# Opening loads in the order in which they land, and the last shift group formed by VectorE from transposed weights

## The chip, the cores and the metric

The kernel runs on one core of a Trainium2 chip. A core has engines that run side by side, each through its own list of instructions in order: TensorE (PE in the profile; PEld is its weight load), VectorE (DVE), ScalarE (ACT), GpSimd (POOL) and SyncE (SP), which here only issues transfers. Transfers run on 16 DMA engines. The metric is the time of the device for one execution, in microseconds (us), as the median of several.

## The reference

One layer of a diffusion backbone for 256 latent tokens `x` with 256 context tokens `ctx`, width 2048. What matters here is its head: each stream is normalised, scaled and shifted by columns that come from a conditioning vector, and then projected.

```python
def modulate(x, g, shift, scale):
    return rms_norm(x, g) * (1 + scale) + shift
...
mod_x = jnp.split((jax.nn.silu(c) @ w_mod[l] + b_mod[l])[:, None, :], 6, axis=-1)
mod_c = jnp.split((jax.nn.silu(c_ctx) @ w_mod[l] + b_mod[l])[None, None, :], 6, axis=-1)
...
qa, ka, va, qb, kb, vb, rb, gf, gb, gate_a, gate_b = proj(modulate(x, g_mix[l], mod_x[0], mod_x[1]))
... = proj(modulate(ctx, g_mix[l], mod_c[0], mod_c[1]))
```

Part 0 of `mod` is the shift, part 1 the scale, each of 2048 channels and for two vectors (`c` for the latent stream, `c_ctx` for the context). `proj(h)` is `h @ w_in`, 2048 by 13344. After it follow windowed attention, gated linear attention, the merge, and a ConvFFN, none of which the change touches.

## The kernel before

Channels lie on partitions: 2048 channels are 16 tiles of 128 (`KT = 16`), and a tile of the normalised input is 128 channels by 256 tokens. Every product is made of three: weights and inputs are split into a high part (`whi`, written by ScalarE, L211) and a remainder (`wlo`, formed by VectorE from the weights and `whi`, L212); high times high, high times low and low times high are summed.

The head of the kernel goes through the 16 channel tiles in five groups: `GROUPS = [(0, 2), (2, 2), (4, 4), (8, 4), (12, 4)]`. For a group, the shift and scale columns of its channels must be there (`mods`), then the input is scaled (`affine_scale`, VectorE) and shifted and split (`affine_shift`: ScalarE writes `h..hi` at L511, VectorE writes `h..lo` at L512), and then TensorE multiplies the group's rows of `w_in` for the q block of the linear attention (`QB`, two projections of 512 columns, latent tokens only), the k block (`KB`, both streams) and the v block (`VB`, both streams). Sums go on over the groups: what a projection leaves in its bank is added by VectorE to `qb`, `kb` or `vb` (L521), and a bank can be used again when that is done. Weights come in chunks of 256 rows by 512 columns (512 KB, a buffer `raw` of a pool of seven). A group of four tiles has eight chunks: QB 1 to 4, KB 5 and 6, VB 7 and 8. For a chunk TensorE first does the products with `whi`, then those with `wlo`.

Shift and scale of a group are computed while the products of the group before run (for the first group, in the opening). One part of one group is `mod_both`: TensorE multiplies the vectors `cS` (32 columns, of which two are used) with `w_mod`, in steps of one 1 MB buffer `mraw` each, four steps for a group of four tiles, into a bank `pm`; VectorE transposes it (`mtr`, L335), TensorE gathers it into columns (`pcol`), VectorE copies those (L345) and adds the bias (L348). Such steps stand in a list, `bg_steps`, and are taken up at the start of chunks at a given rate. While the second group's products run, the places are written out instead (`steps`, `also`, `mid`). `mraw` and the arrays of the head share a pool of 16 buffers (`M`), of which six are left for `mraw` up to the fourth group and two in it.

All these loads are issued by SP in one chain (`load`), in the order in which the program asks for them, and each waits until its buffer is free. In the opening, `pack` (constants, biases and the two vectors in one array) and `crow` (the vector as rows) are issued from ScalarE's queue. Everything that starts needs `pack`: the identity for TensorE's warming transposes (`idle`), and the vectors for `cS`.

For other parts of `mod` (2 to 5) the kernel already has a second way, `mod_latent`: VectorE multiplies a tile of transposed weights (128 channels by 1024) with the vector as a row on all partitions (`csrow`, read back from `csd`) and sums along the row (L376).

A scheduler of the recording layer sets the order on each engine from dependencies and its own estimates. `in_order` and `pin` add orders without a wait.

Of the kernel before, what the change touches and what calls it, by code (L numbers as in the profile page):

```python
# [16 lines left out]
P = 128  # L17
D = 2048
# [13 lines left out]
def layer_kernel(ctx, tc, A, out):  # L32
# [17 lines left out]
    def M(name, shape, dt=F32):  # L50
        return big.tile(shape, dt, name=name, tag="M")
# [62 lines left out]

    pack = cst.tile([P, 322], F32, name="pack")
    nc.scalar.dma_start(pack, A["k_pack"])
    crow = sm.tile([KT, P], F32, name="crow", tag="t128", bufs=2)
    nc.scalar.dma_start(crow, A["k_crow"])
    ident, c1, sel = pack[:, 0:128], pack[:, 128:256], pack[:, 256:290]
# [17 lines left out]
    csd = dram.tile([KT, P], F32, name="csd")  # L137
    G.dma_start(csd, crow)
# [174 lines left out]
    def mod_both(part, t0, n, dst, put=None):  # L313
# [5 lines left out]
        def step(k0):  # L319
            if k0 == 0:  # L320
                a.append(bank(f"pm{part}_{t0}", (P, w), side=True))
            raw = M("mraw", [P, nk, w])
            src = A["w_mod01"][part, t0 + k0 // nk].rearrange("p (c d) -> p c d", c=nk)
            if t0 < 4 and part == 0 and k0:
                load(raw[:, 0:nk // 2, :], src[:, 0:nk // 2, :])
                load(raw[:, nk // 2:nk, :], src[:, nk // 2:nk, :])
            else:
                load(raw, src)
            for k in range(nk):
                kt = k0 + k  # L330
                q = 32 * (kt % 4)
                mm_b(a[0][q:q + 32, :], cS[:, kt, :], raw[:, k, :], start=(kt < 4), stop=(kt >= 12))
            if k0 == KT - nk:
                tr = W2("fb", "mtr", [P, n, 4, 32])
                folded[:] = [V.transpose(tr.rearrange("p a b c -> p (a b c)"), a[0]).ins]  # L335
                a.append(tr)
                if put is not None:
                    put(end)
# [14 lines left out]
    def mod_latent(parts, begin=None):  # L353
# [16 lines left out]
        def step(i):  # L370
# [8 lines left out]
            if begin is not None and i == 0:  # L379
# [27 lines left out]
    def rms_scale(ss, n, shape):  # L407
# [16 lines left out]
            for (t0, n), put in zip(groups, [None, None] + [lambda fn: pend.append(fn)] + 2 * [lambda fn: defer(0, fn)])]  # L424
    pend = []

    rrow1 = []
    kbt = M("kb0", [P, 4, 512])
    vb0 = M("vb0", [P, 4, 512])

    def square_sums(s):
# [3 lines left out]
        for i in range(4):  # L435
# [6 lines left out]
            else:  # L442
                V.tensor_tensor(q, x_, x_, op=ALU.mult)
                parts.extend(q[:, k, :] for k in range(4))
# [97 lines left out]
    V.tensor_scalar(gm1, gmix, -0.5, None, op0=ALU.mult)  # L542
# [73 lines left out]
    for gi, (t0, n) in enumerate(groups):  # L616
# [8 lines left out]
        if gi + 1 < len(groups):  # L625
            bg_steps.extend(mods[gi + 1][0] + mods[gi + 1][1])
            ticks = 4 * ((n + 1) // 2)
            bg_rate[:] = [1.4 * len(bg_steps) / ticks + 0.01, 0.0]
            if gi == 1:
                bg_rate[:] = [0.0, 0.0]  # L630
                steps = iter([1, 2, 1, 4, 0, 0])

# [8 lines left out]

                also = iter([next_columns] * 3 + [scale_2, next_columns, lambda: affine_shift(0, *groups[2])])

# [722 lines left out]
```

## Time and profile before

| | us |
|---|---|
| median of 3 runs | 1973.95 (1973.88 to 1974.18) |
| the profiled execution | 1973.72 |
| its span, first to last instruction | 1972.0 |
| TensorE busy in the span | 1952.8 |
| TensorE busy from 0 to 24 us | 16.21 |

In the profile a row of the timeline or of the chain starts with its time from the start of the span. `xN` is the number of instructions in it; one matrix product in 32-bit floats shows as two of them, so a step of four products of `mod_both` is a row of `pm` x8. What stands behind `<-` in square brackets ended the idle time of the engine just before. TensorE's busy time includes ends that are modelled, so a busy TensorE is not one at its peak.

### The profile page before, as it was taken

The numbers are of one execution on the slowest core, as the hardware profiler recorded it, in microseconds if no ns is written. First come the engines' busy times: TensorE is split into PE (matmuls) and PEld (weight loads), VectorE is DVE, ScalarE is ACT, GpSimd is POOL, SyncE is SP. The second block draws the span as 40 slices with busy tenths as digits, with TensorE's granted clock in tenths as the row PEclk, the third lists the DMA queues.
The fourth block names the chain that finished last, engine by engine and source line by source line (L and its number), as shares of the span: only waits on it lengthen the run. The fifth ranks groups of instructions, "written<-read, shape, count | busy, mean of one in ns | idle before, by whom it ended". The sixth has DMA issues, their size and how long they took to land.

```text
span 1972.0 us, 27091 instructions
## 1 busy us (share of the span) xinstructions
PE 1952.8 (99%) x10304; PEld 1635.6 (83%) x10304; DVE 1396.9 (71%) x2150; ACT 971.6 (49%) x1415; POOL 39.9 (2%) x60
## 2 busy tenths in 40 slices
PE   8999999999999999999999999999999999999999
PEld 6679988888887777888888888888888888888887
DVE  5756855785768998777776467989886545677754
ACT  5223655462346565444444445755555334555533
POOL 0010000020000000000000000000000000000000
PEclk9999999999999999999999999999999999999999
DMA  9975222226654466899997677688786556666563
GB/s 392 412 255 176 69 66 71 79 84 210 212 162 126 129 208 220 297 299 307 312 310 237 238 246 252 193 276 284 263 275 224 192 193 191 186 188 191 188 212 114
DMA packets 182867, 420.90 MB, mean 213 GB/s; under 512 B 12512, under 2 KB 12736, under 8 KB 177744
## 3 DMA queue, kind: packets, MB, share of 16 engines
q1 hardware_dynamic: 181200, 413.45, 63.7%
q0 software_dynamic: 1360, 5.54, 1.0%
q8 instruction: 81, 1.33, 0.3%
q14 instruction: 50, 0.41, 0.1%
q10 hardware_dynamic: 176, 0.17, 0.0%
HBM read 416.98 MB, written 2.13 MB: 213 GB/s over the span
## 4 chain that ended last, share of the span: by engine, by line
PE 94%; DVE 3%; ACT 1%; DMA 1%; issue 1%; ACTq 0%; DVEq 0%
PE acc L83 72%; PE accs L83 12%; PE pa L95 2%; PE poa L95 1%; PE pS L95 1%; PE po L95 1%; PE pm L95 1%; DVE wlo L212 1%; PE ptp L98 1%; DMA mraw<-in_w_mod 1%; ACT whi L211 0%; DVE q L831 0%; PE pto L98 0%; DMA pack<-in_k_pack 0%; DVE k L838 0%
## 5 line engine op out<-in xcount | busy, mean ns | idle before, releaser
L212 DVE TENSOR_TENSOR wlo<-raw,whi 128x1024 fp32r<-128x1024 f32 x568 | 694.0, 1223 | 426.5 <-ACT whi L211 387.8
L211 ACT ACTIVATE whi<-raw 128x1024 fp32r<-128x1024 f32 x568 | 601.1, 1059 | 785.1 <-PE acc L83 605.0
L83 PE MATMUL accs<-h,whi 128*128 128x512 f32 x704 | 176.3, 392 | 0.0
L83 PE MATMUL acc<-h,whi 128*128 128x512 f32 x640 | 160.4, 392 | 0.0
L83 PEld LDWEIGHTS accs<-h,whi 128*128 128x128 f32 x704 | 126.6, 189 | 22.6
L83 PE MATMUL acc<-whi,h01hi 128*128 128x512 f32 x352 | 139.7, 397 | 0.0
L83 PE MATMUL acc<-whi,h00hi 128*128 128x512 f32 x352 | 139.2, 395 | 0.0
L83 PE MATMUL acc<-whi,h01lo 128*128 128x512 f32 x352 | 138.4, 393 | 0.0
L83 PE MATMUL acc<-whi,h00lo 128*128 128x512 f32 x352 | 137.6, 391 | 0.0
L83 PE MATMUL acc<-whi,al 128*128 128x512 f32 x352 | 137.0, 389 | 0.0
L83 PE MATMUL acc<-whi,ah 128*128 128x512 f32 x352 | 137.0, 389 | 0.0
L83 PEld LDWEIGHTS acc<-h,whi 128*128 128x128 f32 x640 | 115.1, 189 | 20.6
L83 PEld LDWEIGHTS accs<-h,wlo 128*128 128x128 f32 x704 | 96.0, 190 | 6.9
L83 PE MATMUL acc<-wlo,h01hi 128*128 128x512 f32 x352 | 99.0, 396 | 0.0
L83 PE MATMUL accs<-h,wlo 128*128 128x256 f32 x704 | 98.2, 282 | 0.0
L83 PE MATMUL acc<-wlo,h00hi 128*128 128x512 f32 x352 | 98.1, 394 | 0.0
L83 PE MATMUL acc<-wlo,ah 128*128 128x512 f32 x352 | 94.3, 389 | 0.0
L83 PEld LDWEIGHTS acc<-h,wlo 128*128 128x128 f32 x640 | 87.4, 190 | 6.3
L83 PE MATMUL acc<-h,wlo 128*128 128x256 f32 x640 | 89.4, 282 | 0.0
L376 DVE CUSTOM_DVE_ANT_0 raw<-raw,csrow,pack 128x1024 f32<-128x1024 f32 x64 | 81.2, 1278 | 0.0
L83 PEld LDWEIGHTS acc<-whi,al 128*128 128x128 f32 x352 | 66.1, 188 | 13.7
L83 PEld LDWEIGHTS acc<-whi,ah 128*128 128x128 f32 x352 | 66.1, 188 | 13.7
(376 smaller groups left out, 3553.0 us busy)
## 6 DMA issues: line engine op xcount, KB each, us to landing
raw<-in_w_in SPq DMA_DIRECT2D x204, 512.0 KB, 4.5
raw<-in_w_up SPq DMA_DIRECT2D x176, 512.0 KB, 4.2
raw<-in_w_modT SPq DMA_DIRECT2D x128, 512.0 KB, 4.6
raw<-in_w_down SPq DMA_DIRECT2D x88, 512.0 KB, 3.6
mraw<-in_w_mod SPq DMA_DIRECT2D x30, 1024.0 KB, 12.5
raw<-in_w_attn_o SPq DMA_DIRECT2D x32, 512.0 KB, 5.3
raw<-in_w_gla_o SPq DMA_DIRECT2D x32, 512.0 KB, 5.4
raw<-in_w_out SPq DMA_DIRECT2D x32, 512.0 KB, 4.4
```

The source lines that it names most:

```text
L83: r = pe_seq(PE.matmul(*a, **k))
L95: return pe_seq(after(PE.matmul(*a, **k)))
L98: return pe_seq(after(PE.transpose(*a)))
L211: j = S.activation(hi[:, 0:n, :], raw[:, 0:n, :], AF.Copy).ins
L212: i = V.tensor_tensor(lo[:, 0:n, :], raw[:, 0:n, :], hi[:, 0:n, :].bitcast(F32), op=ALU.subtract).ins
L376: i0 = V.tensor_tensor_reduce(out=raws[i], in0=raws[i], in1=row[0], scale=1.0, scalar=d if h else bmod[:, b0:b0 + 1], op0=ALU.mult, op1=AL ...
```

## The change

Opening. The vectors get a small array of their own, `ccol`, which is issued first, then `crow` (now with both vectors, 32 rows), then `pack` without the vectors. The 1 MB loads of the first two groups' shift are no longer cut in halves. The first half of the first scale (`a0`) stands ahead of the last three sums of squares instead of behind `factor_row`. 14 of the 32 warming transposes are left out (`idle`).

Second group. Of the four `mod_both` steps of the third group's shift that stood in one place, the last stands one place later, and so does its gathering.

Third and fourth group. The fifth group's shift (channel tiles 12 to 15) is not formed by `mod_both` any more, but by `shift_rows`: for each half of the 2048 input rows, both vectors are read as rows onto all partitions (`c2row`, two transfers of 512 KB into an `M` buffer), and for each of the four tiles a 512 KB tile of transposed weights is loaded into a `raw` buffer and multiplied and summed by VectorE twice, once per vector. The first half stands among the third group's products, the second among the fourth's.

```diff
-    pack = cst.tile([P, 322], F32, name="pack")
+    ccol = cst.tile([P, KT, 2], F32, name="ccol")
+    nc.scalar.dma_start(ccol.rearrange("p k s -> p (k s)"), A["k_ccol"])
+    crow = sm.tile([2 * KT, P], F32, name="crow", tag="t128", bufs=2)
+    nc.scalar.dma_start(crow, A["k_crow"])
+    pack = cst.tile([P, 290], F32, name="pack")
     nc.scalar.dma_start(pack, A["k_pack"])
-    crow = sm.tile([KT, P], F32, name="crow", tag="t128", bufs=2)
-    nc.scalar.dma_start(crow, A["k_crow"])
...
-    S.activation(cS[:, :, 0:2], pack[:, 290:322].rearrange("p (k s) -> p k s", s=2), AF.Silu)
+    S.activation(cS[:, :, 0:2], ccol, AF.Silu)
...
             raw = M("mraw", [P, nk, w])
-            src = A["w_mod01"][part, t0 + k0 // nk].rearrange("p (c d) -> p c d", c=nk)
-            if t0 < 4 and part == 0 and k0:
-                load(raw[:, 0:nk // 2, :], src[:, 0:nk // 2, :])
-                load(raw[:, nk // 2:nk, :], src[:, nk // 2:nk, :])
-            else:
-                load(raw, src)
+            load(raw, A["w_mod01"][part, t0 + k0 // nk].rearrange("p (c d) -> p c d", c=nk))
...
+    def shift_rows():
+        rows = []
+        def half(h):
+            rows[:] = [M("c2row", [P, 2, 1024])]
+            for s in range(2):
+                k = s * KT + 8 * h
+                load(rows[0][:, s, :], csd[k:k + 8, :].rearrange("k p -> (k p)").partition_broadcast(P))
+        def step(h, j):
+            raw = wr.tile([P, 2, 512], F32, name="raw", tag="raw").rearrange("p a b -> p (a b)")
+            prod = f2.tile([P, 1024], F32, name="prod", tag="mod", bufs=1)
+            load(raw, A["w_modT0"][h, j - 12])
+            for s in range(2):
+                d = shift1[:, s, j:j + 1]
+                i = V.tensor_tensor_reduce(out=raw if s else prod, in0=raw, in1=rows[0][:, s, :], scale=1.0,
+                                           scalar=d if h else bmod[:, j:j + 1],
+                                           op0=ALU.mult, op1=ALU.add, accum_out=d).ins
+                in_order(last_lo[0], i)
+        return [[lambda h=h: half(h)] + [lambda h=h, j=j: step(h, j) for j in range(12, 16)] for h in range(2)]
...
-    idle(10)
+    idle(8)
     pr, add_up = square_sums(0)
     add_up(0, 6)
...
+    a0()
     add_up(6, 9)
     factor_row(pr)
-    a0()
-    idle(6)
     a1()
-    idle(4)
+    idle(2)
     ea()
     b0()
     affine_scale(0, *groups[0])
-    idle(6)
+    idle(4)
     b1()
...
-            bg_steps.extend(mods[gi + 1][0] + mods[gi + 1][1])
+            if gi < 2:
+                bg_steps.extend(mods[gi + 1][0] + mods[gi + 1][1])
+            elif gi == 2:
+                first, both = by_rows.pop(0), mods[3][0] + mods[3][1]
+                bg_steps.extend(first[0:1] + both[0:4])
+                for pair in zip(first[1:], both[4:]):
+                    bg_steps.extend(pair)
+            else:
+                first, both = by_rows.pop(0), mods[4][0]
+                bg_steps.extend(first[0:1])
+                for pair in zip(both, first[1:]):
+                    bg_steps.extend(pair)
...
-                steps = iter([1, 2, 1, 4, 0, 0])
+                steps = iter([1, 2, 1, 3, 1, 0])
```

What this moves shows in the order of the built programs. First place: TensorE at the end of the second group, from the last `whi` products of its KB chunk to the start of the third group (`pm_4` is the third group's shift, `pm_8` the fourth's scale). Before:

```order
L95 MATMUL pm_4_693<-mraw,cS 32x512 x16
L83 MATMUL acc<-h00hi,wlo 128x256
...
L83 MATMUL acc<-h10hi,wlo 128x256
L95 MATMUL pcol_4_740<-mtr,pack 32x32
L83 MATMUL acc<-whi,h00hi 128x512
...
L83 MATMUL acc<-wlo,h00hi 128x512 x4
L83 MATMUL acc<-wlo,h10hi 128x512 x4
L95 MATMUL pm_8_793<-mraw,cS 32x512 x4
```

and of the change:

```order
L95 MATMUL pm_4_681<-mraw,cS 32x512 x12
L83 MATMUL acc<-h00hi,wlo 128x256
...
L83 MATMUL acc<-h10hi,wlo 128x256
L95 MATMUL pm_4_681<-mraw,cS 32x512 x4
L83 MATMUL acc<-whi,h00hi 128x512
...
L95 MATMUL pcol_4_752<-mtr,pack 32x32
L83 MATMUL acc<-wlo,h00hi 128x512 x4
L83 MATMUL acc<-wlo,h10hi 128x512 x4
L95 MATMUL pm_8_784<-mraw,cS 32x512 x4
```

The fourth step of `pm_4` now stands behind the KB chunk's `wlo` products, and the gathering behind the VB chunk's `whi` products. At the same place, ScalarE; the last of the `whi` ahead of the `h00hi` is, before, that of the third group's first chunk. Before:

```order
L511 ACTIVATE h10hi<-xr_87,shift_101 128x256 x2
L211 ACTIVATE whi<-raw 128x1024 x3
L511 ACTIVATE h00hi<-xr_85,shift_101 128x256 x4
L511 ACTIVATE h10hi<-xr_87,shift_101 128x256 x4
L211 ACTIVATE whi<-raw 128x1024 x7
```

and of the change:

```order
L534 ACTIVATE h10hi<-xr_89,shift_103 128x256 x2
L213 ACTIVATE whi<-raw 128x1024 x2
L534 ACTIVATE h00hi<-xr_87,shift_103 128x256 x4
L534 ACTIVATE h10hi<-xr_89,shift_103 128x256
L213 ACTIVATE whi<-raw 128x1024
L534 ACTIVATE h10hi<-xr_89,shift_103 128x256 x3
```

The first chunk's `whi` now stands behind five writes of `h..hi`, which wait for the gathered shift.

Second place: VectorE in the third group, from the sums of its first QB block into `qb` to the `wlo` of the fourth chunk. Before:

```order
L521 TENSOR_TENSOR qb_252<-qb_252,acc 128x512
L521 TENSOR_TENSOR qb_253<-qb_253,acc 128x512
L335 STREAM_TRANSPOSE mtr<-pm_8_793 128x512
L212 TENSOR_TENSOR wlo<-raw,whi 128x1024
L345 COPY scale_102<-pcol_8_914 32x2x4 x4
L348 TENSOR_TENSOR scale_102<-scale_102,pack 128x2x4
L499 SCALAR_TENSOR_TENSOR scale_102<-scale_102,gm_100 128x4 x2
L502 SCALAR_TENSOR_TENSOR xr_86<-xr_86,scale_102,rrow 128x256 x2
L212 TENSOR_TENSOR wlo<-raw,whi 128x1024
```

and of the change (the ISA rows of `prod` and `raw` are the new multiply-and-sums, the ISA rows with `shift_103` alone the reading of the sum), up to the third chunk's `wlo`:

```order
L544 TENSOR_TENSOR qb_241<-qb_241,acc 128x512
L544 TENSOR_TENSOR qb_242<-qb_242,acc 128x512
L401 ISA prod,shift_103<-raw,c2row,pack 128x1024
L401 ISA shift_103 128x1
L332 STREAM_TRANSPOSE mtr<-pm_8_784 128x512
L401 ISA raw,shift_103<-raw,c2row,pack 128x1024
L401 ISA shift_103 128x1
L214 TENSOR_TENSOR wlo<-raw,whi 128x1024
```

and from there to the fourth chunk's:

```order
L342 COPY scale_104<-pcol_8_910 32x2x4 x4
L345 TENSOR_TENSOR scale_104<-scale_104,pack 128x2x4
L401 ISA prod,shift_103<-raw,c2row,pack 128x1024
L401 ISA shift_103 128x1
L522 SCALAR_TENSOR_TENSOR scale_104<-scale_104,gm_102 128x4 x2
L401 ISA raw,shift_103<-raw,c2row,pack 128x1024
L401 ISA shift_103 128x1
L525 SCALAR_TENSOR_TENSOR xr_88<-xr_88,scale_104,rrow 128x256 x4
L525 SCALAR_TENSOR_TENSOR xr_90<-xr_90,scale_104,rrow 128x256 x4
L214 TENSOR_TENSOR wlo<-raw,whi 128x1024
```

Two multiply-and-sums stand ahead of each of these two `wlo`, and all eight scalings of `xr` (before: two) ahead of the second.

Third place: VectorE in the fourth group, of the change, from the `wlo` of its fourth chunk to the sums of the second QB block:

```order
L214 TENSOR_TENSOR wlo<-raw,whi 128x1024
L401 ISA prod,shift_103<-raw,c2row,shift_103 128x1024
L401 ISA shift_103 128x1
L401 ISA raw,shift_103<-raw,c2row,shift_103 128x1024
L401 ISA shift_103 128x1
L214 TENSOR_TENSOR wlo<-raw,whi 128x1024
L544 TENSOR_TENSOR qb_243<-qb_243,acc 128x512
L544 TENSOR_TENSOR qb_244<-qb_244,acc 128x512
```

and before:

```order
L212 TENSOR_TENSOR wlo<-raw,whi 128x1024
L502 SCALAR_TENSOR_TENSOR xr_86<-xr_86,scale_102,rrow 128x256 x2
L502 SCALAR_TENSOR_TENSOR xr_88<-xr_88,scale_102,rrow 128x256 x2
L521 TENSOR_TENSOR qb_254<-qb_254,acc 128x512
L521 TENSOR_TENSOR qb_255<-qb_255,acc 128x512
```

The sums of the second QB block, which free the banks of the KB chunks, stood right behind four scalings; now two multiply-and-sums and a `wlo` stand ahead of them.

More of the change, by code (lines that the diff above doesn't have):

```diff
@@ L136, in layer_kernel @@
         S.preload_act_table_set("natural_log_exp_and_others")
-    csd = dram.tile([KT, P], F32, name="csd")
+    csd = dram.tile([2 * KT, P], F32, name="csd")
     G.dma_start(csd, crow)
@@ L425, in layer_kernel @@
     pend = []
+    by_rows = shift_rows()
     rrow1 = []
@@ L429, in layer_kernel @@
     vb0 = M("vb0", [P, 4, 512])
+    squared = []
     def square_sums(s):
@@ L442, in square_sums @@
             else:
-                V.tensor_tensor(q, x_, x_, op=ALU.mult)
+                squared.append(V.tensor_tensor(q, x_, x_, op=ALU.mult).ins)
                 parts.extend(q[:, k, :] for k in range(4))
@@ L640, in scale_2, with shift_2 @@
                         affine_scale(s, *groups[2])
-                also = iter([next_columns] * 3 + [scale_2, next_columns, lambda: affine_shift(0, *groups[2])])
+                def shift_2():
+                    next_columns()
+                    affine_shift(0, *groups[2])
+                also = iter([next_columns] * 3 + [scale_2, next_columns, shift_2])
                 def mid():
@@ L1345 @@
     c, c_ctx = data.pop("c")[0], data.pop("c_ctx")
-    data["k_crow"] = c.reshape(KT, P)
+    data["k_crow"] = np.concatenate([c.reshape(KT, P), c_ctx.reshape(KT, P)])
+    data["w_modT0"] = w_mod[:, 12 * P:D].T.reshape(4, P, 2, 1024).transpose(2, 0, 1, 3)
     data["k_pack"] = np.concatenate(
         [consts.pop("k_ident")] + [col(data.pop(n)[0]) for n in ("b_mod", "g_mix", "g_ffn")]
-        + [consts.pop("k_sel"), np.stack([col(c), col(c_ctx)], axis=2).reshape(P, 2 * KT)], axis=1)
+        + [consts.pop("k_sel")], axis=1)
+    data["k_ccol"] = np.stack([col(c), col(c_ctx)], axis=2).reshape(P, 2 * KT)
     conv = data.pop("conv_w")[0]
```

2 lines of the change are left out of this document (1 added, 1 removed).

## The prediction

> **What bounds the kernel now.** The page first, for who is busy; then the waits of TensorE over the head, since the change touches nothing behind it; then the chain of work, the timeline of the engines that TensorE waits for, and the transfers.
>
> ```profile
> PE 1952.8 (99%) x10304; PEld 1635.6 (83%) x10304; DVE 1396.9 (71%) x2150; ACT 971.6 (49%) x1415; POOL 39.9 (2%) x60
> 0.00:24.00 24.00, 16.21 (x127) 10.96 (x128) 10.31 (x30) 9.09 (x13) 0.82 (x5) 1.00 0.93 369
> 70.00:83.00 13.00, 13.00 (x84) 9.95 (x84) 9.36 (x21) 6.38 (x11) 0.00 (x0) 1.00 1.02 409
> 83.00:95.00 12.00, 11.77 (x96) 7.43 (x94) 9.12 (x21) 2.58 (x3) 0.00 (x0) 1.00 1.03 407
> PE pm L95 <- DMA mraw<-in_w_mod: 1.2, 1, 1.2
> ```
>
> TensorE is idle 19.2 of 1972 us, 7.8 of them in the first 24. After that a microsecond less or more on TensorE is one of the whole. But in the stretches of the third group (70 to 95 us) VectorE is busy 9 of 12 or 13 us (the third figure behind the length) and the DMA engines all the time (share 1.02). This head has three resources near their limit, and the change takes from one and gives to the other two.
>
> The opening hangs on landings. TensorE's last step for the first shift and its first product, and ScalarE's first `whi`:
>
> ```profile
> 19.94 1.07 PE L95 MATMUL pm<-mraw,cS 128*32 128x256 f32 x16
> 20.78 1.06 ACT L211 ACTIVATE whi<-raw 128x1024 fp32r<-128x1024 f32 x1 [4.71 <-DMA raw<-in_w_first]
> 23.30 0.39 PE L83 MATMUL acc<-h00hi,whi 128*128 128x256 f32 x1 [0.46 <-ACT h00hi L511]
> ```
>
> The 512 KB that landed at 20.78 had one 1 MB load of this shift right ahead of it.
>
> How fast loads land in the third group, and what the products take, by the waits of ScalarE and by the chain:
>
> ```profile
> 70.42 1.06 ACT L211 ACTIVATE whi<-raw 128x1024 fp32r<-128x1024 f32 x1 [17.55 <-DMA raw<-in_w_in]
> 71.58 1.71 ACT L511 ACTIVATE h00hi<-xr,shift 128x256 fp32r<-128x256 f32 x4
> 95.89 1.06 ACT L211 ACTIVATE whi<-raw 128x1024 fp32r<-128x1024 f32 x1 [0.29 <-DMA raw<-in_w_in]
> ...
> 55.59 10.88 DMA mraw<-in_w_mod
> 66.52 1.07 PE pm L95 x8
> 67.58 2.10 PE acc L83 x16
> ...
> 69.86 5.67 PE acc L83 x24
> 75.52 0.99 PE pm L95 x8
> 76.52 3.07 PE acc L83 x24
> 83.65 1.85 PE pm L95 x16
> 95.11 5.94 PE acc L83 x48
> ```
>
> Between the first and the last `whi` ten MB were issued (seven `mraw`, six `raw`): 2.55 us a MB. A `mod_both` step costs TensorE 1.0 us, two in a row 1.85, a QB chunk 3.07 (its `whi` products some 1.95 of it), a KB chunk 5.94.
>
> VectorE between the first QB block and the fourth chunk, and what its `wlo` meet on TensorE; then the new operation as the kernel already has it elsewhere:
>
> ```profile
> 83.21 1.28 DVE L521 TENSOR_TENSOR qb<-qb,acc 128x512 f32<-128x512 f32 x2 [3.78 <-PE acc L83]
> 85.57 0.72 DVE L335 STREAM_TRANSPOSE mtr<-pm 128x512 f32<-128x512 f32 x1 [1.07 <-PE pm L95]
> 86.21 1.18 DVE L212 TENSOR_TENSOR wlo<-raw,whi 128x1024 fp32r<-128x1024 f32 x1
> 88.87 0.67 DVE L345 COPY scale<-pcol 32x8 f32<-32x8 f32 x4 [1.48 <-PE pcol L95]
> 89.97 0.88 DVE L502 SCALAR_TENSOR_TENSOR xr<-xr,scale,rrow 128x256 f32<-128x256 f32 x2
> 90.77 1.22 DVE L212 TENSOR_TENSOR wlo<-raw,whi 128x1024 fp32r<-128x1024 f32 x1
> 91.91 1.67 DVE L502 SCALAR_TENSOR_TENSOR xr<-xr,scale,rrow 128x256 f32<-128x256 f32 x4
> 87.44 1.21 PE L83 MATMUL acc<-h00hi,wlo 128*128 128x256 f32 x8
> 92.04 1.21 PE L83 MATMUL acc<-h00hi,wlo 128*128 128x256 f32 x8 [0.23 <-DVE wlo L212]
> 453.59 1.27 DVE L376 CUSTOM_DVE_ANT_0 raw<-raw,csrow,pack 128x1024 f32<-128x1024 f32 x1
> 454.79 1.28 DVE L376 CUSTOM_DVE_ANT_0 raw<-raw,csrow,pack 128x1024 f32<-128x1024 f32 x1
> ```
>
> Already before, a `wlo` ends at 87.39 and 91.99 and TensorE takes it up 0.05 us later: VectorE has no slack at these two places. One multiply-and-sum follows the other after 1.20 us, an `xr` scaling after 0.40, a `wlo` after 1.15.
>
> **The change, part by part.** The sum is against the profiled execution's 1973.72 us (span 1972.0), 0.23 below the median of the runs.
>
> *Opening.* `ccol` lets ScalarE start before `pack` has landed, but the last 1 MB load ahead of the `w_first` chunk lands at 20.78 - 0.5 x 2.55 = 19.5 as before; `cS` and the sums move into the time before it. So the step at 19.94 can start 0.4 us earlier at most: -0.35 (between -0.4 and +1.1, see the third rival).
>
> *Second group.* TensorE waits 1.2 us at 66.5 for the last `mraw` of the third group's shift. Now the 2.1 us of `wlo` products stand ahead of this step: it is reached at 67.1 and the load is there. -1.2. The 0.35 above stays, since 67.1 is still behind the landing.
>
> *Removed.* Four steps and one gathering of the fifth group's shift in the fourth group, and a wait of 0.27 there for a `wlo` behind the scale columns:
>
> ```profile
> 137.57 1.21 PE L83 MATMUL acc<-h01hi,wlo 128*128 128x256 f32 x8 [0.27 <-DVE wlo L212]
> 138.78 1.85 PE pm L95 x16
> 146.59 1.00 PE pm L95 x8
> 153.53 0.18 PE pcol L95 x2
> ```
>
> 1.85 + 2 x 1.0 + 0.15 + 0.27 = -4.25.
>
> *Loads.* By the order of SP, 2.5 MB more stand ahead of the third group's first KB weights (`c2row` 1, three transposed tiles 1.5), and 1 MB ahead of its first chunk. From 66.47, at 2.55 a MB, the first four chunks land at 72.9, 79.2, 84.3 and 92.0. The `whi` products need them, ScalarE's 1.06 included, from about 75.5, 80.5, 84.5 and 91.9 (times below): just enough. 0, up to +1 if the broadcast rows take longer.
>
> [...] The windows show 407 and 409 GB/s here, so the trace decides for 2.55.
>
> *Third group, first chunk.* Its `whi` now waits behind five `h..hi`, which wait for the gathered shift. From the gathering's end: VectorE's copies 0.65, one sum of `vb` 0.6, bias 0.2, five `h..hi` 2.0, `whi` 1.06, in all 4.6 with hand-overs; TensorE has 1.9 of `wlo` products and a step 1.0 until it needs it. +1.75 (1 to 2).
>
> *Third chunk.* Counted from W, the end of the second chunk (83.65 before): two sums of `qb` from W-0.44, 1.2 apart in all; multiply-and-sum 1.2; `mtr` 0.64; multiply-and-sum 1.2; `wlo` 1.22: W+5.05. TensorE is there at W + 1.0 (one step, before two) + 1.95 = W+2.95. +2.15 (1.5 to 2.5).
>
> *Fourth chunk.* Its columns are gathered after the third chunk's `wlo` products: at W+6.3. Then copies and bias from W+6.5 to W+7.3, multiply-and-sum 1.2, factor 0.2, multiply-and-sum 1.2, eight `xr` at 0.4, `wlo` 1.22: W+14.35. TensorE is there at W+6.45 + 1.85 + 1.95 = W+10.25. +4.15, less the 0.23 waited before: +3.9 (3 to 5). Before, two scalings alone stood ahead.
>
> The other two pairs of the third group run beside the KB chunks, of which TensorE has 5.94 us each.
>
> *Fourth group, fifth chunk.* TensorE has the third bank of KB to write 1.95 into it, which VectorE frees with the sum of the second QB block. From the end of the second chunk to there TensorE needs 2 steps + 2 chunks + 1.95 = 10.1; VectorE needs (rows below for the prices) the sums of the first block to +0.75, four scalings into `h11lo` 1.6, four multiply-and-sums 4.8, three `wlo` 3.45, one sum 0.7: 11.3. +1.2 (0 to 2).
>
> ```profile
> 128.68 1.28 DVE L521 TENSOR_TENSOR qb<-qb,acc 128x512 f32<-128x512 f32 x2 [5.98 <-PE acc L83]
> 129.88 1.27 DVE L512 SCALAR_TENSOR_TENSOR h11lo<-xr,shift,h11hi 128x256 fp32r<-128x256 f32 x3
> ```
>
> *Fifth group.* Its scale is gathered at the start of VB instead of 19 us before, with 11 us of VB products as cover; the constants that wait on GpSimd for this scale come as much later, and are first used some 40 us on. 0.
>
> Sum: -0.35 - 1.2 - 4.25 + 1.75 + 2.15 + 3.9 + 1.2 = +3.2. **1973.72 + 3.2 = 1976.9 us**, 0.16% slower: TensorE is given 5.8 us and waits 9.0 for VectorE and ScalarE.
>
> **The rivals.**
>
> *First: the queues hold no one up* (faster). If the products ahead cover VectorE after all, since TensorE's ends are modelled and the third group starts with `whi` and `wlo` further ahead than I reckon, only the gains count: 1973.72 - 5.8 = 1967.9; half of the waits gives 1972.4. For it: VectorE has in all 25% free there. Against it: both `wlo` were taken up within 0.05 us before, and each has 2.4 us and more in front of it now. It decides when less than 2.0 of the 9.0 us are left.
>
> *Second: the loads of `c2row` are slow* (slower). All 128 partitions read the same 4 KB.
>
> ```profile
> raw<-in_w_modT SPq DMA_DIRECT2D x128, 512.0 KB, 4.6
> DMA to landing us min/median/max: 5.0/5.6/6.5
> ```
>
> The second row is that of `csrow`, such a broadcast of 512 KB: 1.0 us above weights of the same size. If that is a longer hold of the engines and not a latency, two of them put every later load back by 2.0 us, and the second chunk's `whi` waits 1.0: 1977.9. If it takes its 5.6 instead of 1.28 us, landings slip by 8.6 and W by 7.4: 1984.3. From 2 us of slip on it is slower than can be told from no change.
>
> *Third: TensorE slows down in the opening.* Warming transposes at the start and later:
>
> ```profile
> 6.74 2.14 PEld L535 LDWEIGHTS warm<-pack 128*128 128x128 f32 x10
> 21.75 0.86 PEld L535 LDWEIGHTS warm<-pack 128*128 128x128 f32 x8
> ```
>
> 0.21 us against 0.11 each: TensorE starts at half speed. With 14 transposes fewer, and waits for landings of up to 2 us in their place, it could be slow again at 23 us. A spell as long as the row's 2.14 us loses 1.1, and the second group's slack is used up by then: 1978.0. Against it: the products around the waits go on, and the granted clock is 1.00 in each window. [...]
>
> **How the numbers follow.** About 0.2%, 3.95 us, is what a measurement of this kernel can tell from no change: below 1970.0 is faster, above 1977.9 slower. The sum's case has 0.62; its own range, by the bounds of the four waits, is 1974 to 1979.5, with a quarter of it above 1977.9. The first rival has 0.13, most of it below 1970.0; the second 0.14, from 1977.9 up; the third 0.11, about half above. So faster 0.11, slower 0.155 + 0.14 + 0.06, with some for waits I don't see: 0.39; within 0.2% the rest, 0.50. The range that leaves out the better half of the first rival and the worse half of the second is 1971.0 to 1981.5.
>
> **What would show it.** In the changed profile: no wait for `mraw` at 66 us; the first product of the head near 22.9; TensorE idle before the third group's first `whi` products (about 1.7 us, by ScalarE), before the `wlo` products of its third (2.1) and fourth chunk (4, by VectorE), and in the fourth group's fifth chunk before the third bank (1); 32 fewer `pm` instructions; from there on the same rows, some 3 us later. Wrong would make it: `wlo` rows that end early at these places (first rival), waits for `raw` or `c2row` instead (second), 0.39 us rows among the first products in numbers (third).

## The result, and the profile after

The changed kernel takes **1981.87 us** (1981.35 to 1983.31 in 5 runs) against 1973.95: the ratio is 1.0042, with a 95% interval of 1.0031 to 1.0053. It is slower by 7.9 us, where 3.0 were forecast, and 0.4 us beyond the end of the range. The profiled execution took 1981.35 us with a span of 1979.6, 7.6 more than the one before.

First the page's line of busy times, then the waits of TensorE over the head (what waited, for whom: us in total, how often, the longest):

```profile
PE 1951.0 (99%) x10258; PEld 1634.7 (83%) x10258; DVE 1414.6 (71%) x2176; ACT 970.9 (49%) x1415; POOL 40.1 (2%) x60
PE warm L561 <- DMA pack<-in_k_pack: 9.8, 1, 9.8
PE acc L83 <- DVE wlo L214: 4.4, 2, 2.4
PE pcol L95 <- DVE mtr L332: 1.7, 2, 1.3
PE acc L83 <- ACT whi L213: 1.6, 1, 1.6
PE acc L83 <- DVE qb L544: 1.1, 1, 1.1
```

Before, the same view began with

```profile
PE warm L538 <- DMA pack<-in_k_pack: 6.7, 1, 6.7
```

TensorE is busy 1.8 us less than before, and yet the end comes later. The wait for `mraw` (1.2) is gone. The three waits that the prediction named are there: `whi` 1.6, `wlo` twice, the third bank 1.1. But the first row has grown from 6.7 to 9.8, the waits for `mtr` from 0.4 to 1.7, and something is missing from this list, since it is no wait. TensorE's timeline shows it:

```profile
25.18 0.38 PE L83 MATMUL acc<-h00hi,whi 128*128 128x256 f32 x1 [0.46 <-ACT h00hi L534]
...
41.41 0.23 PE L95 MATMUL pcol<-mtr,pack 128*32 128x16 f32 x2 [0.42 <-DVE mtr L332]
42.31 0.38 PE L83 MATMUL acc<-h10hi,whi 128*128 128x256 f32 x1 [0.67 <-ACT h10hi L534]
...
43.46 0.41 PE L83 MATMUL acc<-h10hi,whi 128*128 128x256 f32 x1
43.67 0.42 PE L83 MATMUL acc<-h10lo,whi 128*128 128x256 f32 x1
...
94.83 3.48 PE L95 MATMUL pm<-mraw,cS 128*32 128x512 f32 x13
```

From 43.46 on the same products start 0.21 us apart instead of 0.12, and the two `pm` steps at 94.7 take 3.5 us instead of 1.85. The windows around these places give the granted clock, the third figure from the end (ahead of it stand the length and the busy times of PE, PEld, DVE, ACT and POOL, behind it the share of the DMA engines and GB/s):

```profile
40.04:43.45 3.41, 2.18 (x26) 1.12 (x19) 3.13 (x11) 0.91 (x2) 0.00 (x0) 1.00 1.05 386
43.46:46.86 3.40, 3.40 (x21) 2.86 (x24) 2.30 (x9) 0.00 (x0) 0.00 (x0) 0.50 1.06 425
77.58:81.00 3.42, 1.81 (x14) 0.69 (x13) 3.42 (x8) 3.42 (x8) 0.00 (x0) 1.00 1.00 403
91.24:94.65 3.41, 1.46 (x12) 1.17 (x10) 2.26 (x3) 1.06 (x1) 0.00 (x0) 1.00 1.01 406
94.65:98.06 3.41, 3.41 (x19) 0.83 (x18) 2.93 (x10) 1.06 (x1) 0.00 (x0) 0.50 1.04 415
```

Twice TensorE runs at half its clock, each time for 3.41 us. In the kernel before there is no such stretch between the first product and the end.

Starts of the same work in both timelines show where the time went (us; the last column is what the step added):

| first product of | before | after | later by | step adds |
|---|---|---|---|---|
| the head | 23.30 | 25.18 | 1.88 | 1.88 |
| the second group's first chunk | 48.31 | 51.69 | 3.38 | 1.50 |
| `wlo`, last chunk of the second group | 73.55 | 75.76 | 2.21 | -1.17 |
| third group, first chunk | 76.45 | 80.47 | 4.02 | 1.81 |
| third group, third chunk, `wlo` | 87.44 | 93.56 | 6.12 | 2.10 |
| third group, fifth chunk | 95.04 | 104.97 | 9.93 | 3.81 |
| fourth group, fifth chunk | 140.57 | 146.41 | 5.84 | -4.09 |
| fourth group, sixth chunk | 147.51 | 154.64 | 7.13 | 1.29 |
| fifth group | 164.65 | 171.78 | 7.13 | 0 |

The remaining 0.5 us of the 7.6 come little by little in the 1800 us behind, which the change doesn't touch; no single row shows them.

TensorE's step behind the second chunk, then VectorE in the third group, whose rows answer to those shown of before:

```profile
88.44 1.06 PE L95 MATMUL pm<-mraw,cS 128*32 128x512 f32 x8
88.07 1.28 DVE L544 TENSOR_TENSOR qb<-qb,acc 128x512 f32<-128x512 f32 x2 [3.43 <-PE acc L83]
89.27 1.28 DVE L401 CUSTOM_DVE_ANT_0 prod<-raw,c2row,pack 128x1024 f32<-128x1024 f32 x1
91.11 1.24 DVE L401 CUSTOM_DVE_ANT_0 raw<-raw,c2row,pack 128x1024 f32<-128x1024 f32 x1
92.28 1.22 DVE L214 TENSOR_TENSOR wlo<-raw,whi 128x1024 fp32r<-128x1024 f32 x1
98.40 3.25 DVE L525 SCALAR_TENSOR_TENSOR xr<-xr,scale,rrow 128x256 f32<-128x256 f32 x8
101.57 1.22 DVE L214 TENSOR_TENSOR wlo<-raw,whi 128x1024 fp32r<-128x1024 f32 x1
```

That step starts 0.07 us ahead of the modelled end of the second chunk, as before (83.58, with W = 83.65), so W is 88.51. The two `wlo` end at 93.50 and 102.79, which is W + 4.99 and W + 14.28; the prediction had W + 5.05 and W + 14.35.

### The profile page after: what moved, and what is told of

Same layout as the page of the kernel before. It is cut to its first block, busy times and chain, and to the rows that moved or that the text cites. A ratio compares the mean times of both kernels' runs of the same rounds, so it can differ in the third digit from the quotient of the medians.

```text
span 1979.6 us, 27033 instructions
## 1 busy us (share of the span) xinstructions
PE 1951.0 (99%) x10258; PEld 1634.7 (83%) x10258; DVE 1414.6 (71%) x2176; ACT 970.9 (49%) x1415; POOL 40.1 (2%) x60
## 4 chain that ended last, share of the span: by engine, by line
PE 67%; DVE 1%; ACT 0%; issue 0%
PE acc L83 52%; PE accs L83 12%; PE poa L95 1%; PE pS L95 1%; PE ptp L98 1%; PE pto L98 0%; DVE wlo L214 0%; PE ptx L98 0%; ACT s L1069 0%; ACT whi L213 0%; DVE s L1074 0%; PE ptq L98 0%; DVE yd L1321 0%; DVE yd L1315 0%; DVE sq L1003 0%
## 5 line engine op out<-in xcount | busy, mean ns | idle before, releaser
L83 PEld LDWEIGHTS acc<-whi,h00hi 128*128 128x128 f32 x352 | 66.4, 189 | 14.1 <-issue 0.8
```

What stands on the lines that cost most here:

```text
L83: r = pe_seq(PE.matmul(*a, **k))
```

## The experiments

The kernel before gave medians of 1974.10 to 1974.20 beside these.

**The opening alone, and all but the opening.** The first takes the changed kernel and gives it the old shift and the old places of the second group:

```diff
-            if gi < 2:
-                bg_steps.extend(mods[gi + 1][0] + mods[gi + 1][1])
-            elif gi == 2:
...
+            bg_steps.extend(mods[gi + 1][0] + mods[gi + 1][1])
-                steps = iter([1, 2, 1, 3, 1, 0])
+                steps = iter([1, 2, 1, 4, 0, 0])
```

> The kernel before with the changed opening alone (the fifth group's shift by mod_both again, the four steps of the second group in their old places). Theory: the opening itself costs, since pack is now the third transfer of its queue and lands 3.1 us later (9.8 against 6.7 us), and TensorE's first work waits for it; the first product stands 1.9 us later: 1973.95 + 1.9 = 1975.9, and 1.4 more (1977.3) if TensorE falls to half clock near 43 us as in the changed kernel. Rival: the opening costs nothing and all 7.9 us come from the shift by rows: 1973.9.

Measured: 1976.05 us (ratio 1.0011, 1.0002 to 1.0019). The second takes back the opening's lines and leaves the rest (`crow` keeps both vectors, which the new shift needs):

```diff
-    ccol = cst.tile([P, KT, 2], F32, name="ccol")
-    nc.scalar.dma_start(ccol.rearrange("p k s -> p (k s)"), A["k_ccol"])
+    pack = cst.tile([P, 322], F32, name="pack")
+    nc.scalar.dma_start(pack, A["k_pack"])
     crow = sm.tile([2 * KT, P], F32, name="crow", tag="t128", bufs=2)
     nc.scalar.dma_start(crow, A["k_crow"])
-    pack = cst.tile([P, 290], F32, name="pack")
-    nc.scalar.dma_start(pack, A["k_pack"])
...
-    idle(8)
+    idle(10)
...
-    a0()
     add_up(6, 9)
     factor_row(pr)
+    a0()
+    idle(6)
```

> The changed kernel with the opening of before (pack first and whole, 32 warming transposes, the half a0 behind factor_row, the 1 MB loads cut in halves). Theory: 1.9 less by the opening, and 1.4 less if the half-clock spell near 43 us hangs on where the opening leaves TensorE: 1981.9 - 3.3 = 1978.6; without the second, 1980.0. The waits of the third group stay: 1.6 for whi, 2.0 and 2.4 for wlo. Rival: the opening costs nothing: 1981.9.

Measured: 1978.73 us (1.0022, 1.0013 to 1.0031). So the opening costs 2 us by itself and 3.1 on top of the rest, and what is left costs 4.6. Part of the 2 us is half clock: five of the eleven executions of the first, from 1975.58 to 1975.86, have a granted clock of 1.000, and the profiled one, with the spell, took 1976.92. In the profile of the first, TensorE's first product stands at 25.77, and from 44.65 on its products start 0.21 us apart instead of 0.12; coming later, TensorE no longer waits for `mraw` at 66 us, which gives 1.2 us back. The profiled execution of the second (1977.35) has a granted clock of 0.999, that of the changed kernel 0.998.

**What in the opening costs.** Turning round the order of the three small transfers:

```diff
+    pack = cst.tile([P, 290], F32, name="pack")
+    nc.scalar.dma_start(pack, A["k_pack"])
     ccol = cst.tile([P, KT, 2], F32, name="ccol")
...
-    pack = cst.tile([P, 290], F32, name="pack")
-    nc.scalar.dma_start(pack, A["k_pack"])
```

> The changed kernel with one thing turned round: pack is issued ahead of ccol and crow. Theory (the order of the three transfers is what costs): pack lands near 6.6 us, TensorE starts 3 us earlier, the first product stands near 23.3 instead of 25.2: 1981.9 - 1.9 = 1980.0, and 1.4 less if the spell near 43 us goes too. Rival (the missing transposes or the half of the scale that stands between the sums of squares cost it): the first product stays near 25.2, 1981.9.

Measured: 1982.39 us (1.0042, 1.0030 to 1.0055). My theory failed here: TensorE starts at 6.37, and the first product still stands at 25.12. ScalarE's and TensorE's timelines of this kernel say why:

```profile
8.94 1.28 ACT L135 ACT_TABLE_LOAD   x1 [8.94 <-DMA ccol<-in_k_ccol]
11.98 2.95 ACT L462 ACTIVATE sq<-xr 128x1024 f32<-128x1024 f32 x3
13.81 1.13 PE L485 MATMUL pr<-sq,ones 128*128 128x256 f32 x4 [3.16 <-DVE sq L470]
```

Now `ccol` is the late one. ScalarE's first work needs it, and its squares (`sq`), which need nothing of it, stand behind that work, so TensorE's sums are as late as in the changed kernel. The transfers' times from issue to landing, of the changed kernel and then of this one:

```profile
pack<-in_k_pack ACTq DMA_DIRECT2D x1, 145.0 KB, 8.1
ccol<-in_k_ccol ACTq DMA_DIRECT2D x1, 16.0 KB, 5.1
crow<-in_k_crow ACTq DMA_DIRECT2D x1, 16.0 KB, 5.5
```

```profile
pack<-in_k_pack ACTq DMA_DIRECT2D x1, 145.0 KB, 5.6
ccol<-in_k_ccol ACTq DMA_DIRECT2D x1, 16.0 KB, 7.7
crow<-in_k_crow ACTq DMA_DIRECT2D x1, 16.0 KB, 8.0
```

The next kernel has the new order of TensorE's work in the opening, the missing transposes and the uncut loads, but the vectors in `pack` again, which is first; shift and second group as before:

```diff
-    S.activation(cS[:, :, 0:2], ccol, AF.Silu)
+    S.activation(cS[:, :, 0:2], pack[:, 290:322].rearrange("p (k s) -> p k s", s=2), AF.Silu)
```

> The kernel before with the changed opening, but pack whole and first, then crow, as before: of the opening only the order of TensorE's work (half of the first scale ahead of the last sums of squares), the uncut loads and the 14 missing transposes are left. Theory: two things cost in the opening, the third transfer of the small queue that lands at 9 us or later whichever it is, and the half step (1.0 us) ahead of the sums; with the queue as before only the second is left, less what stood behind: first product 0.3 earlier to 1.0 later than 23.3, 1974 to 1976. Rival (the missing transposes cost the clock): first product 1.9 later and 1976 as with the whole opening.

Measured: 1973.33 us (0.9997, 0.9987 to 1.0006), with a granted clock of 1.000 in the profiled execution and an early first product:

```profile
22.81 0.39 PE L83 MATMUL acc<-h00hi,whi 128*128 128x256 f32 x1 [0.46 <-ACT h00hi L532]
```

Beside the whole opening's 1976.05, the separate array `ccol` costs 2.7 us by the medians, and 2.3 to 2.5 beside its executions at clock 1.000. That holds in both orders tried: ahead of `pack` it delays TensorE (first instruction at 9.81 instead of 6.68), behind `pack` it delays ScalarE (8.94 instead of 6.71). The rest of the opening costs nothing, and may gain half a microsecond. The rival with the transposes is out; by the traces it is 12 of 39 that are missing (27 are left), not 14 of 32.

**The half clock.** Ten warming transposes fill TensorE's two short waits at 41 and 42 us:

```diff
-            pc = bank(f"pcol{part}_{t0}", (32, n * 4, 2), side=True)
+            fill = t0 == 2 and part == 1
+            whole = bank(f"pcol{part}_{t0}", (P, 512) if fill else (32, n * 8), side=True)
+            pc = whole[0:32, 0:n * 8].rearrange("p (a c) -> p a c", c=2)
+            for _ in range(4 if fill else 0):
+                pe_seq(PE.transpose(whole[:, 256:256 + P], ident, ident))
             mm_b(pc, sel[:, 0:32], a[1].rearrange("p a b c -> p (a b) c")[:, :, 0:2], start=True, stop=True)
+            for _ in range(6 if fill else 0):
+                pe_seq(PE.transpose(whole[:, 256:256 + P], ident, ident))
```

> The changed kernel with ten warming transposes on TensorE in its two short waits at 41 to 42 us, four ahead of the gathering of the second group's scale and six behind it. Theory: the half clock from 43.46 to 46.86 comes from too little work in the 3.41 us ahead of it; with 1.1 us of transposes in there it stays away, and 1.4 us go: 1980.5. The second spell, at 94.65, stays, or costs nothing, since VectorE is what TensorE waits for there. Rival: the spell has another cause, the row of 0.41 us products stays and the time with it: 1981.9.

Measured: 1981.78 us (1.0042, 1.0029 to 1.0054): no gain. The first spell stayed away in the execution profiled, and yet the time is the same. TensorE's timeline and windows:

```profile
42.30 0.38 PE L83 MATMUL acc<-h10hi,whi 128*128 128x256 f32 x1
...
43.44 0.28 PE L83 MATMUL acc<-h10hi,whi 128*128 128x256 f32 x1
101.25 1.83 PE L83 MATMUL acc<-h00hi,wlo 128*128 128x256 f32 x8 [4.00 <-DVE wlo L214]
103.00 1.94 PE L95 MATMUL pm<-mraw,cS 128*32 128x512 f32 x8
98.16:101.57 3.41, 0.32 (x2) 0.33 (x3) 3.41 (x7) 0.00 (x0) 0.00 (x0) 1.00 1.02 384
101.57:104.98 3.41, 3.41 (x17) 1.52 (x15) 3.37 (x7) 2.12 (x2) 0.00 (x0) 0.50 1.04 401
```

The product at 43.44 takes 0.28 us, where the changed kernel's at 43.46 takes 0.41, and the second group's first chunk starts at 50.17 instead of 51.69. But in the third group the second spell, too, falls elsewhere. In the changed kernel it came at 94.65, ahead of the 2.42 us wait for `wlo`: it only shortened that wait, and cost nothing. Here the wait is 4.00 us in one piece, and the spell comes behind it, on work that nothing covers. The fifth chunk starts at 104.87 (104.97 in the changed kernel).

**The second group's step moved, alone.** The kernel before, with this line of the change:

```diff
-                steps = iter([1, 2, 1, 4, 0, 0])
+                steps = iter([1, 2, 1, 3, 1, 0])
```

> The kernel before with one thing changed on the engines: the fourth mod_both step of the third group's shift and its gathering stand one place later (crow has both vectors, which the shift by rows would need, and nothing uses them). Theory: TensorE no longer waits 1.2 us for mraw near 66 us, but ScalarE's whi of the third group's first chunk now stands behind five h..hi that wait for the gathering, 1.6 to 1.7 us: 1974.1 + 0.5 = 1974.6. Rival: the wait for whi comes only with the loads of the shift by rows, and the move alone gains: 1972.9.

Measured: 1974.37 us (1.0002, 0.9993 to 1.0011). The time is near my theory's, the mechanism is the rival's. ScalarE's rows in this kernel:

```profile
70.56 1.06 ACT L211 ACTIVATE whi<-raw 128x1024 fp32r<-128x1024 f32 x1 [16.05 <-DMA raw<-in_w_in]
76.79 1.71 ACT L537 ACTIVATE h00hi<-xr,shift 128x256 fp32r<-128x256 f32 x4 [5.17 <-DVE shift L348]
```

The first chunk's `whi` is done at 71.6, almost six microseconds before TensorE's first product of that chunk (77.35): without the loads of the shift by rows the scheduler leaves it ahead of the `h..hi`, and TensorE waits there only 0.2 us, for `h00hi`. That the move of the step alone puts `whi` behind was wrong. The move still costs something there, by another way: from the start of the second group's last `whi` products to the third group's second chunk TensorE takes 12.0 us (70.00 to 81.97) where it took 10.7 before (69.79 to 80.51), since the gathering now stands in that stretch and the first products follow the `h..hi` one by one. In the profiled execution (1975.23) the 1.2 us gained at 66 us went there, and on top of that its granted clock is 0.999, where the six executions up to 1974.38 have 1.000.

**The shift by rows, alone.** The changed kernel with the old opening and, by this line, the old places:

```diff
-                steps = iter([1, 2, 1, 3, 1, 0])
+                steps = iter([1, 2, 1, 4, 0, 0])
```

> The changed kernel with the opening of before and the four steps of the second group in their old places, so that the shift by rows is all that is left. Theory: against the kernel with the old opening alone (1978.7) the wait for whi (1.6) goes and that for mraw (1.2) comes back: 1978.3; the waits for wlo at the third and fourth chunk of the third group (2.0 and 2.4) stay. Rival: with the loads of c2row ahead, TensorE finds no weights and waits longer than 1.2 at 66 us: 1979 or more.

Measured: 1978.39 us (1.0022, 1.0013 to 1.0032), with waits of 1.4 for `mraw`, 4.8 for `wlo` (3.2 the longest) and 1.1 for `qb`. So 4.2 us belong to the shift by rows; the granted clock of the profiled execution (1978.26) is 0.999.

**Which VectorE work makes the wait.** The same kernel, with six of the eight scalings of `xr` behind the fourth chunk's `wlo`, where they stood before:

```diff
             i = V.scalar_tensor_tensor(xk, xk, scale1[:, s, kt:kt + 1], rrow1[s], op0=ALU.mult, op1=ALU.mult).ins
+            if t0 == 8 and (s or kt > 9):
+                in_order(lo4[0], i)
```

> The kernel with the shift by rows alone, in its places beside the QB chunks (1978.4), with all but two of the eight scalings ordered behind the wlo of the third group's fourth chunk. Theory: of the 3.2 us of waiting for this wlo 2.4 are the six scalings, and the half-clock spell that follows that wait goes with it: 1978.4 - 2.4 - 1.5 = 1974.5, or 1976.0 if a spell stays somewhere. Rival (the two multiply-and-sums ahead make the wait, the scalings would be covered): 1978 or more.

Here `lo4[0]` is that `wlo`. Measured: 1974.99 us (1.0005, 0.9996 to 1.0015), 3.4 less. TensorE's wait for this `wlo` falls from 3.20 to 1.03 us, about the price of six scalings (2.4). So the scalings that the scheduler had put in front, and not only the multiply-and-sums, were what TensorE waited for. Both profiled executions have a granted clock of 0.999, and between them the gain is 2.4 us (1978.26 and 1975.86).

**The multiply-and-sums beside the long chunks.** Opening and second group are those of before. Each pair stands at a chunk of its own, from the fifth on (`at_tick` is a list that `tick` takes up, one entry at each chunk):

```diff
+            bg_steps.extend(mods[gi + 1][0] + mods[gi + 1][1] if gi < 3 else mods[4][0])
+            if gi > 1:
+                rows = by_rows.pop(0)
+                at_tick[:] = [[], [], [], rows[0:1]] + [[r] for r in rows[1:]]
```

> Opening and second group as before; the fifth group's shift by rows, but its multiply-and-sums stand beside the KB and VB chunks of the third and the fourth group (ticks 5 to 8), of which TensorE has 5.4 to 5.9 us each, and none beside the QB chunks of 3.07 us. Theory (the place of VectorE's work is what costs, not its amount): no wait for wlo above 0.3 us in the third group, no half clock, and the four steps are gained: 1974.1 - 4.25 = 1969.8, 1971 if a third-bank wait of 1.1 us stays. Rival (VectorE or the loads are short in the whole of both groups): the waits move to the KB chunks and the time stays at 1976 or above.

Measured: 1974.34 us (1.0000, 0.9991 to 1.0009), 4.0 less than beside the short chunks and 4.5 more than expected. Its rows:

```profile
90.13 3.26 DVE L531 SCALAR_TENSOR_TENSOR xr<-xr,scale,rrow 128x256 f32<-128x256 f32 x8
93.31 1.22 DVE L215 TENSOR_TENSOR wlo<-raw,whi 128x1024 fp32r<-128x1024 f32 x1
94.58 1.22 PE L83 MATMUL acc<-h00hi,wlo 128*128 128x256 f32 x8 [2.62 <-DVE wlo L215]
95.73 3.36 PE L95 MATMUL pm<-mraw,cS 128*32 128x512 f32 x16
```

No multiply-and-sum stands ahead of the fourth chunk's `wlo` any more, but all eight scalings still do; TensorE waits 2.62 for them and then takes 3.36 us for two steps, which take 1.85 at full clock. With the scalings ordered as above, and the multiply-and-sums where this trace showed VectorE free:

```diff
+                half, *four = by_rows.pop(0)
+                where = (3, 4, 5, 7, 7) if gi == 2 else (0, 1, 2, 4, 5)
+                at_tick[:] = [[fn for w, fn in zip(where, [half] + four) if w == t] for t in range(8)]
```

> As the kernel with the late multiply-and-sums (opening and second group as before), with two things more: of the eight xr scalings for the fourth group all but two are ordered behind the wlo of the third group's fourth chunk, as they stood before, and the multiply-and-sums stand where the trace of that kernel shows VectorE free (third group: fifth, sixth and twice eighth chunk; fourth group: second, third, fifth, sixth). Theory: in that kernel 2.6 us of waiting for this wlo, by 2.4 us of scalings ahead of it, and 1.6 us of a half-clock spell right behind it ate the gain; without both 1974.3 - 2.3 - 1.6 = 1970.4. Rival (VectorE's total is what is short): the waits come back at the KB or VB chunks and it stays within 1 us of 1974.

Measured: 1971.80 us (0.9988, 0.9980 to 0.9997). The same with the opening that had given 1973.33:

> The same with the opening's new order of TensorE's work and the uncut loads, but pack whole and first (alone this gave 1973.3). Theory: the two gains add up, less what the wait for mraw near 66 us takes back of an earlier start (that load is bound by the transfers): 1969.6 to 1970.4. Rival: the earlier start is lost whole to that wait, or the idle stretches of the opening cost a half-clock spell of 1.5: 1970.4 to 1972.

Measured: **1971.44 us** (0.9986, 0.9977 to 0.9995), faster than both kernels. Both profiled executions have a granted clock of 1.000, and the runs of each lie within 0.6 us, while those of the changed kernel spread over 2.0. What stays is 1.5 us for a `wlo` in the fourth group, behind two pairs of multiply-and-sums. Moving them further back there:

```diff
-                where = (3, 4, 5, 7, 7) if gi == 2 else (0, 1, 2, 4, 5)
+                where = (3, 4, 5, 7, 7) if gi == 2 else (0, 1, 4, 5, 7)
```

> As the kernel with the late multiply-and-sums and the new opening order (1971.4), with those of the fourth group at its second, fifth, sixth and eighth chunk instead of second, third, fifth and sixth. Theory: the 1.5 us that TensorE waits there for the wlo of the third chunk (two pairs of multiply-and-sums ahead of it) goes, and nothing else changes: 1970.0 to 1970.6. Rival: the pair that moves behind stands ahead of the sums of kb, which free the banks of the VB chunks, and costs as much there: 1971.4.

Measured: 1971.81 us (0.9989, 0.9980 to 0.9998): the rival. TensorE's waits in this kernel:

```profile
PE acc L83 <- DVE kb L548: 1.7, 1, 1.7
PE pm L95 <- DMA mraw<-in_w_mod: 0.6, 1, 0.6
PE acc L83 <- DVE wlo L215: 0.2, 1, 0.2
```

The wait of 1.5 us for a `wlo` is gone, and 1.7 us for the banks of `kb` are there instead. The profiled execution, 1973.08, with a granted clock of 0.999, is one of three above 1973 us; the eight others, from 1971.40 to 1971.96, gain nothing either.

## Why the prediction was wrong

Its sum was +3.2, and the head gave +7.1. Step by step:

- *Opening*: -0.35 was reckoned, +1.88 measured. This is the step that failed: that "the last 1 MB load ahead of the `w_first` chunk lands" at 19.5 as before, and "the step at 19.94 can start 0.4 us earlier at most". It took for granted that the loads of the shift were what the opening waits for. In the changed kernel TensorE never waits for them: `pack`, now third in its queue, landed 3.1 us later, TensorE's first instruction and with it the sums of squares waited for it, and the chain from the sums over the factor row to the first gathering set the end. The first operation of the factor row and the first gathering, before and then in the changed kernel:

```profile
14.75 0.42 DVE L471 TENSOR_SCALAR vrow<-pr 128x256 f32<-128x256 f32 x1 [1.22 <-PE pr L462]
18.09 0.20 PE L95 MATMUL pcol<-mtr,pack 128*32 128x16 f32 x1
```

```profile
17.54 0.43 DVE L494 TENSOR_SCALAR vrow<-pr 128x256 f32<-128x256 f32 x1 [4.80 <-PE pr L485]
20.19 0.20 PE L95 MATMUL pcol<-mtr,pack 128*32 128x16 f32 x1 [1.32 <-DVE mtr L332]
```

I had credited the early `ccol` to ScalarE and never asked what becomes of the transfers behind it; its price, 2.3 to 2.7 us by the two kernels with and without it, is above even the upper bound of +1.1 that I gave.
- *Half clock*: not in the sum, +1.50 measured. The third rival had the right effect at the wrong place: I looked for it at 23 us, behind the missing transposes, and held against it that the products around the waits go on. It came at 43.46, behind two waits of 0.42 and 0.67 us that the kernel before has as well (0.4 and 0.7).
- *Wait for `mraw`*: -1.2 reckoned, -1.17 measured, but this agreement proves little. The moved step does away with the wait, as the kernel with the old opening shows; so does a TensorE that comes more than 1.2 us later to it, as the kernel with the opening alone shows. In the changed kernel both hold, and the 1.2 us are gained once.
- *The other terms*: *First chunk, `whi`*: +1.75 and +1.81 (ScalarE's order, as reckoned, but it comes with the new loads and not with the moved step alone). *Third chunk*: +2.15 and +2.10. *Fourth chunk*: +3.9 and +3.81. *Removed steps*: -4.25 and -4.09. *Fifth chunk of the fourth group*: +1.2 and +1.29. Each of these stands within 0.2 us, with the engine and the row that the prediction named. In the fourth chunk TensorE's wait is only 2.4 of the 4 us, since the second spell slowed the two steps ahead of it; VectorE's end, W + 14.28, set the time either way. Some sums of the prediction are slightly off by its own figures (W+14.35 less W+10.25 is 4.10 and not 4.15, the least sum of the range is 1973.4 and not 1974, the second rival's first wait is 0.7 and not 1.0); none of them decides anything here.
- *Loads*: reckoned as just enough. ScalarE takes up the third and the fourth chunk's weights as they land, at 84.13 and 91.73; 84.3 and 92.0 had been worked out from 2.55 us a MB, the broadcast rows included. So the second rival, broadcasts that hold the engines longer, is out, and the first (the queues hold no one up) by the waits above.

```profile
84.13 1.06 ACT L213 ACTIVATE whi<-raw 128x1024 fp32r<-128x1024 f32 x1 [1.56 <-DMA raw<-in_w_in]
91.73 1.06 ACT L213 ACTIVATE whi<-raw 128x1024 fp32r<-128x1024 f32 x1 [6.54 <-DMA raw<-in_w_in]
```

Of the 3.9 us that the head took more than reckoned, 3.7 are the opening's own term (2.2) and the first spell (1.5). The kernel with the old opening is without the opening's term, and its profiled execution has a granted clock of 0.999 where the changed kernel's has 0.998; it took 1977.35 us, and the prediction's terms without the opening's give 1973.72 + 3.55 = 1977.3. That execution is the fastest of eleven, and the median is 1.4 higher. The two slowest (1979.47 and 1979.53) have a granted clock of 0.998 where the others have 0.999, so further half clock is likely in these; for the others it may be a spell on work that no wait covers, which is not shown.

## What to carry to other kernels

A small transfer put in front of others was paid by what stood behind it (`pack`, behind `ccol` and `crow`, landed 3.1 us later): ask, for each engine, what its first instruction waits for, and follow that chain, not the largest loads. Work moved to VectorE, 71% busy, was free only where TensorE's stretch was long enough: the same eight pairs of multiply-and-sums cost 4.2 us with half of them beside chunks of 3.07 us, and gained 2.3 with most of them beside those of 5.94, once a scheduler's choice (six scalings ahead of a `wlo`) had been taken back. With that choice taken back in both, the places are worth 3.2 us (1974.99 and 1971.80). And idle time on TensorE cost twice, the second time at half clock behind it (with the ten transposes, 4.00 us of waiting and then 3.41 us at a clock of 0.50), at a place that moved from one of these kernels to the next.

## What the runs showed of the hardware

In the profile of the changed kernel the first full clock comes at 12.73, 2.9 us after TensorE's first instruction (9.81): ahead of it products of `pr` start 0.43 us apart, behind it 0.22. In the kernel before it comes at 10.00, 3.3 us after the first instruction (6.68). The changed kernel's two spells begin at 43.45 and 94.65, which is 9 and 24 times 3.413 us after its first full clock, and each lasts 3.413 us; half clock comes once more at 1978.81 (576 times), behind TensorE's last product, and lasts to the end of the span. With ten transposes put into the two waits just ahead of it, the first spell stayed away in the execution profiled. Busy time from the profile doesn't order the cases, since it has modelled ends: 2.18 us in the 3.41 us ahead of a spell, 1.81 in as many without one behind (two of the rows above).

Each matmul can be counted instead with the spacing that it has when work is back to back (0.12 us for a product of the first chunks, 0.43 for four of `mod_both`, which run side by side). Take windows of 3.413 us, counted from the first full clock. In the changed kernel those ahead of the two spells hold 1.2 and 1.1 us of work, by this estimate; the emptiest of the others in the head, at 77.58, holds 1.3, and full clock followed it. In the kernel before the emptiest window of the head has 1.7 (at 37.31), and full clock followed. No wait in the window ahead of the first spell was above 0.67 us.

Executions of one kernel differ in their granted clock; a spell takes 0.0009 off (1.7 of 1975 us), an estimate from its 3.41 us at 0.50. With the opening alone, the five executions up to 1975.86 us have 1.000 and the six from 1976.05 on 0.999; with the step alone, the six up to 1974.38 have 1.000 and the four from 1974.98 on 0.999; the slowest of all, 1985.22 with `pack` first, has 0.996. What decides it is not shown, since only one execution of each was profiled.

Why `ccol`, of 16 KB in 128 rows, lands 7.7 us after its issue when it stands behind `pack`, while `crow`, of 16 KB in 32 rows, took 6.0 at that place in the kernel that has no `ccol` (the one with 1973.33 us), no run here tells.
